# The last projection's last two tiles by three ranges of tokens, and a norm's squares added on VectorE

## The chip, the cores and the metric

The kernel runs on one core of a Trainium2 chip. The metric is the device time of one execution in microseconds, as the median of several runs. TensorE (PE in the profile) multiplies matrices, with a second row, PEld, for the loads of its stationary operand; VectorE is DVE, ScalarE is ACT, GpSimd is POOL, and SyncE (SP) issues most transfers. Each engine works through its own list of instructions in order; semaphores hold it where an operand is not there yet.

## The reference, cut to what matters

Two transformer blocks run one after the other on 512 tokens of 1024 channels. The change lies in the second block's feed-forward part:

```python
x = x + rms_norm(merged @ w_out[l], norm_mix_post[l])
h = rms_norm(x, norm_ffn_pre[l])                 # the squares of x are summed here
u = causal_dwconv(h @ w_up[l], conv_ffn_w[l])
a, g = jnp.split(u, 2, axis=-1)
f = (jax.nn.gelu(g, approximate=True) * a) @ w_down[l]     # 2816 -> 1024
x = x + rms_norm(f, norm_ffn_post[l])            # the last norm; x is the output
```

`rms_norm` divides each token by the root of the mean of its 1024 squares, so no element of a token can leave before all eight tiles of 128 channels of `f` are known for that token.

## The kernel before, in words

Activations lie transposed: a tile is 128 channels on the partitions by 512 tokens. A projection is cut into output tiles of 128 channels. Each tile sums over `nk` slices of 128 input channels in one PSUM bank; the down projection has `KF` = 22 slices. For accuracy every operand is split in a high and a low half (fp32r), and one slice is three matmuls (`mm3`, lines 163 to 165): high by high, low activation by high weight, high activation by low weight. The weights are the stationary operand (128x128), the activations `act` stream past in columns, one column for each token. Each matmul has its own weight load.

Weights come as pieces into `wraw`. `Stream.hi` lets ScalarE write the high half `whi` (line 201) and VectorE the low half `wlo` (line 209), up to two units ahead of TensorE (`AHEAD`); a unit is 8 or 6 slices of one tile. Nothing reorders this: the order in which the Python code is written is the order on each engine, and generators (`take`, `run`) interleave pieces of it.

The last projection is `ended_by_norm(p_down2, 1, ...)`. Tiles 0 to 6 are computed over all 512 tokens. After each, ScalarE copies the bank to `fo` with the norm's gain (`evac_f`, line 1543), and squares it (`square_o`, line 1473), and GpSimd adds the squares into `ssq` (line 1075). Tile 7 is done by halves of 256 tokens in one bank (`half`). Within the second half stand the sums over channels of the first half's squares (`col_sums`, line 382: matmuls against a column of ones, fp32, two passes each), the root (`rsqrt_col`, lines 319 to 329, VectorE with one square root on ScalarE), and its spread over the partitions (`bcast`, line 390, fp32, two passes for 128 tokens). Then `chain_f` multiplies `fo` by it (line 1550), adds the residual `x1` (line 1554), and sends the pieces out (lines 1556 and 1558). It gives one of the four pairs of tiles to GpSimd, and the second half's chain stands behind the first's. All that follows the last matmul of the second half is the end of the program.

The other place is `squares` (lines 1492 to 1499): between the second block's output projection and its up projection it squares the new `x1` on ScalarE (line 1497) and adds the squares of six tiles for each half of the tokens on GpSimd (line 1499). `start` (line 1503) puts the sums of these (`acc3`, `last3`) on TensorE in the midst of the up projection, and after nine more matmuls the spread root, which all the up projection's evacuations need.

Of the kernel before, what the change touches and what calls it, by code (L numbers as in the profile page):

```python
# [10 lines left out]
F32R = mybir.dt.float32r  # L11
AF = mybir.ActivationFunctionType
# [3 lines left out]
P = 128  # L16
T = 512
# [6 lines left out]
KF = FF // P  # L24
# [110 lines left out]
def program(ctx: ExitStack, tc: tile.TileContext, A, outT):  # L135
    nc = tc.nc
# [13 lines left out]
    def bank(name="bank", cols=T):  # L150
        return ps.tile([P, cols], F32, tag="b", name=name, padded_shape=[P, T])

    def slot(dt=F32, name="slot", cols=T):
        t = sl.tile([P, T], dt, tag="s", name=name)
        return t if cols == T else t[:, :cols]

    def pair(name, cols=T):
        return slot(F32R, name + "_hi", cols), slot(F32R, name + "_lo", cols)


    def mm3(out, lhs, rhs, start, stop, **kw):

        PE.matmul(out, lhs[0], rhs[0], start=start, stop=False, **kw)  # L163
        PE.matmul(out, lhs[0], rhs[1], start=False, stop=False, **kw)  # L164
        PE.matmul(out, lhs[1], rhs[0], start=False, stop=stop, **kw)  # L165
# [10 lines left out]
    class Stream:  # L176


        def __init__(self):
            self.pieces, self.units, self.raw, self.got, self.owed = [], [], [], [], []  # L180
            self.limit = 1 << 30
# [9 lines left out]
        def hi(self, u):  # L191

            while len(self.got) <= min(u, len(self.units) - 1):
                p, ks, cs = self.units[len(self.got)]
                self.load(p + 2)
                src = self.raw[p][:, ks, cs]
                nk, n = src.shape[1:]
                hi = whi_p.tile([P, 1024], F32R, tag="whi", name="whi")
                lo = wlo_p.tile([P, 1024], F32R, tag="wlo", name="wlo")
                h, l = (t[:, : nk * n].rearrange("p (k n) -> p k n", n=n) for t in (hi, lo))  # L200
                S.activation(h, src, AF.Copy)  # L201
                self.got.append((h, l))
                self.owed.append((l, src, h))
# [19 lines left out]
    class Proj:  # L223

        def __init__(self, w, c0, nk, ncol=256, wide=False):
            self.nk, self.at = nk, {}
            first = len(ws.pieces)
            segs = [(k0, min(8, nk - k0)) for k0 in range(0, nk, 8)]  # L230
            ws.pieces += [(w, k0, n, c0, ncol) for k0, n in segs]
            if wide:
                for u in range(0, nk, 4):
                    for k in range(4):
                        self.at[0, u + k] = (len(ws.units), k, 0)
                    ws.units.append((first, slice(u, u + 4), slice(0, ncol)))
                return
            per = 2 if nk <= 4 else 1
            for m in range(0, ncol // P, per):
                for s, (k0, n) in enumerate(segs):  # L240
                    for k in range(n):
                        for q in range(per):
                            self.at[m + q, k0 + k] = (len(ws.units), k, q * P)
                    ws.units.append((first + s, slice(0, n), slice(m * P, (m + per) * P)))
# [11 lines left out]
    def tiles(pj, ms, acts, evac):  # L256

        for m in ms:
            b = bank()
            yield from tile_gen(pj, m, acts, b)  # L260

            ws.hi(ws.early(pj.at[m, pj.nk - 1][0] + 1))
            evac(m, b)
            ws.lo()
            tick()

    def run(gen):
        for _ in gen:
            pass
# [104 lines left out]
    def sqrt_table():  # L374
        S.activation(warm, ones, AF.Sqrt)

    def col_sums(parts, blocks):

        b = bank("sums", cols=len(blocks))
        for i, blk in enumerate(blocks):  # L380
            for j, a in enumerate(parts):
                PE.matmul(b[:, i : i + 1], a[:, blk * P : (blk + 1) * P], ones,  # L382
                          start=(j == 0), stop=(j == len(parts) - 1))
        return b

    def bcast(col, n):

        b = bank("bc", cols=n * P)
        for i in range(n):
            PE.matmul(b[:, i * P : (i + 1) * P], col[:, i : i + 1].to_broadcast([P, P]), ident,  # L390
                      start=True, stop=True)
        return b
# [33 lines left out]
        ])  # L426
    p_out2 = [Proj(A["w_out_2"], 256 * i, 8) for i in range(4)]
    p_up2 = [[Proj(A["w_up_2"], c + 256 * j, 8) for c in (FF, 0)] for j in range(KF // 2)]
    p_down2 = [Proj(A["w_down_2"], 256 * i, KF) for i in range(4)]


    xs = []
# [10 lines left out]
    def pc(name, i, n=1):  # L443
        a = PCOL[name][0]
        return par[:, a + i : a + i + n]
# [613 lines left out]
    ws.limit = 1 << 30  # L1059


    def ended_by_norm(pjs, late, acts, evac, square, chain, follow=None, between=None, begun=(), after=None):


        nk = pjs[0].nk
        acc = slot(name="ssq")
        whole = 8 - late

        def early(m, b, i0):
            i = i0 + m  # L1070
            evac(i, b, slice(0, T))
            t = acc if i == 0 else slot(name="sq")
            square(i, t, b, slice(0, T))
            if i:
                G.tensor_add(acc, acc, t)

        for i, (g, b) in enumerate(begun):
            run(g)
            early(i, b, 0)
            tick()  # L1080
        for i in range(len(begun), whole):
            run(tiles(pjs[i // 2], (i % 2,), acts, lambda m, b: early(i % 2, b, i - i % 2)))
        if between:
            between()
        sqrt_table()
        ends = {i: (bank(), slot(name="sq")) for i in range(whole, 8)}

        def half(ts):
            for i in range(whole, 8):
                b, t = ends[i]  # L1090
                yield from tile_gen(pjs[i // 2], i % 2, acts, b, ts)
                evac(i, b, ts)
                square(i, t, b, ts)

        def sums(hf):
            return rsqrt_col(col_sums([acc] + [ends[i][1] for i in range(whole, 8)], (2 * hf, 2 * hf + 1)), 2)

        n = late * nk
        run(half(HALF[0]))
        g = half(HALF[1])  # L1100
        take(g, max(4, n // 4))
        r = sums(0)
        take(g, max(6, n // 4))
        bc = bcast(r, 2)
        ch = chain(0, HALF[0], bc)
        take(ch, CHN)
        run(g)
        run(ch)
        if follow is None:
            run(chain(1, HALF[1], bcast(sums(1), 2)))  # L1110
            return
        a, b = follow(HALF[0])
        run(a)
        r = sums(1)
        take(b, 4)
        ch = chain(1, HALF[1], bcast(r, 2))
        run(ch)
        if after:
            after(0)
        run(b)  # L1120
        a, b = follow(HALF[1])
        run(a)
        if after:
            after(1)

        ws.limit += 2
        ws.need(ws.limit - 2)
        run(b)
        ws.limit = 1 << 30
# [362 lines left out]
    def squares(hf):  # L1492
        ts = HALF[hf]
        for k in range(8):
            t = acc3 if k == 0 else last3 if k == 7 else slot(name="sq", cols=256)
            t = t[:, ts] if k in (0, 7) else t
            S.activation(t, x1[k][:, ts], AF.Square)
            if 0 < k < 7:
                G.tensor_add(acc3[:, ts], acc3[:, ts], t)  # L1499

    R3 = slot(name="R3")

# [30 lines left out]
    ffn_up(p_up2, (p_out2, 2, mg, evac_o, square_o, chain_o), h2, evac_g2, evac_a2, after=squares, start=start)  # L1533


    fo = {}

    def evac_f(i, b, ts):
        for hf in range(2):
            if ts.start <= HALF[hf].start < ts.stop:  # L1540
                if (i // 2, hf) not in fo:
                    fo[i // 2, hf] = slot(name="fo").rearrange("p (k n) -> p k n", k=2)
                S.activation(fo[i // 2, hf][:, i % 2, :], b[:, HALF[hf]], AF.Copy, scale=pc("norm_ffn_post_2", i))

    def chain_f(hf, ts, rb):
        rbs = slot(name="rbs", cols=256)
        out = outT.rearrange("(k p) n -> p k n", p=P)
        for j, e in ((0, V), (1, V), (3, G), (2, V)):
            f = fo[j, hf]
            e.tensor_mul(f, f, (rbs if j else rb).unsqueeze(1).to_broadcast([P, 2, 256]))  # L1550
            if j == 0:
                S.activation(rbs, rb, AF.Copy)
            for n in range(2):
                e.tensor_add(f[:, n, :], f[:, n, :], x1[2 * j + n][:, ts])
                if j == 2:
                    nc.sync.dma_start(out[:, 4 + n, ts], f[:, n, :])
            if j != 2:
                nc.sync.dma_start(out[:, 2 * j : 2 * j + 2, ts], f)
            yield j + 1

    ended_by_norm(p_down2, 1, act, evac_f, square_o, chain_f)


# [16 lines left out]
```

## Time and profile before

| | |
|---|---|
| median of 3 runs | 1421.41 us (1418.87 to 1423.46) |
| the profiled execution | 1421.66 us, its span 1419.9 us |
| TensorE busy | 1382.8 us, 97% of the span |
| VectorE, ScalarE, GpSimd busy | 55%, 39%, 16% |
| last matmul of the last projection starts | 1405.41 us |
| mean granted TensorE clock | 0.991 of 2.4 GHz |

Times in rows are microseconds from the start of the span. A matmul row's start is when it begins to stream, and the time between two starts is what a matmul costs in a full stream, since the end of one overlaps the next. In square brackets stands the idle time of the engine before the row, and who ended it.

### The profile page before, as it was taken

How to read it: one execution, taken by the hardware profiler on the slowest of the kernel's cores; microseconds unless marked ns; L12 is line 12 of the kernel's file. 1: busy time of each engine (PE TensorE's matmuls, PEld its weight loads, DVE VectorE, ACT ScalarE, POOL GpSimd, SP SyncE). 2: the span in 40 equal slices, each digit the busy share in tenths (PEclk: the TensorE clock that was granted, in tenths of full speed). 3: DMA queues.
4: the chain of work that ended last, by engine and by line, in shares of the span. 5: the costliest groups of instructions: out<-in, count | busy, mean ns of one | idle time of the engine just before them, and what ended most of it. 6: DMA issues, size and time to landing. Idle time of an engine off the chain costs nothing.

```text
span 1419.9 us, 18781 instructions
## 1 busy us (share of the span) xinstructions
PE 1382.8 (97%) x7546; PEld 1166.0 (82%) x7546; DVE 778.9 (55%) x1140; ACT 557.8 (39%) x892; POOL 221.1 (16%) x210
## 2 busy tenths in 40 slices
PE   6999999999999999999999999999999999999996
PEld 4767988899888888888988888888887888888886
DVE  4478777656444433443557874445257866663224
ACT  4433256535333333323345543223454534443321
POOL 0021324111110111112010212000261101110102
PEclk9999999999999999999999999999999999999998
DMA  9993252322322322232274123223311323222221
GB/s 364 342 338 107 78 148 58 121 89 89 119 89 89 119 88 83 82 104 90 59 201 112 60 68 111 89 89 111 98 60 60 119 90 114 94 82 82 93 71 60
DMA packets 141942, 160.42 MB, mean 113 GB/s; under 512 B 5664, under 2 KB 119584, under 8 KB 141856
## 3 DMA queue, kind: packets, MB, share of 16 engines
q1 hardware_dynamic: 140416, 156.91, 33.6%
q10 hardware_dynamic: 1440, 2.31, 0.5%
q8 instruction: 59, 0.97, 0.3%
q14 instruction: 27, 0.22, 0.0%
HBM read 147.67 MB, written 2.10 MB: 105 GB/s over the span
## 4 chain that ended last, share of the span: by engine, by line
PE 86%; DVE 7%; ACT 3%; issue 2%; DMA 1%; POOL 1%; SPq 0%; DVEq 0%; ACTq 0%; POOLq 0%
PE bank L164 24%; PE bank L163 24%; PE bank L165 24%; PE v L163 1%; PE v L165 1%; PE v L164 1%; PE sums L382 1%; PE first L163 1%; DVE wlo L209 1%; PE z L1362 1%; PE first L165 1%; PE first L164 1%; DVE e L887 1%; POOL acc L1499 1%; PE ada L472 1%
## 5 line engine op out<-in xcount | busy, mean ns | idle before, releaser
L209 DVE TENSOR_TENSOR wlo<-wraw,whi 128x1024 fp32r<-128x1024 f32 (+1 forms) x214 | 278.9, 1310 | 141.5 <-ACT whi L201 141.4
L164 PE MATMUL bank<-h_lo,whi 128*128 128x512 f32 (+1 forms) x816 | 306.3, 375 | 0.1
L163 PE MATMUL bank<-h_hi,whi 128*128 128x512 f32 (+1 forms) x816 | 305.7, 375 | 0.0
L165 PE MATMUL bank<-h_hi,wlo 128*128 128x512 f32 (+1 forms) x816 | 304.7, 373 | 0.8 <-DVE wlo L209 0.8
L201 ACT ACTIVATE whi<-wraw 128x1024 fp32r<-128x1024 f32 (+1 forms) x214 | 220.6, 1035 | 121.1 <-PE bank L164 107.0
L163 PEld LDWEIGHTS bank<-h_hi,whi 128*128 128x128 f32 x816 | 153.9, 189 | 30.4 <-PE adab L472 1.7
L165 PEld LDWEIGHTS bank<-h_hi,wlo 128*128 128x128 f32 x816 | 154.0, 189 | 28.6 <-DVE wlo L209 1.6
L164 PEld LDWEIGHTS bank<-h_lo,whi 128*128 128x128 f32 x816 | 153.9, 189 | 28.2 <-DVE h_lo L1490 0.3
L163 PE MATMUL bank<-act_hi,whi 128*128 128x512 f32 (+1 forms) x374 | 141.1, 377 | 0.8 <-ACT sq L1473 0.8
L164 PE MATMUL bank<-act_lo,whi 128*128 128x512 f32 (+1 forms) x374 | 140.8, 376 | 0.0
L165 PE MATMUL bank<-act_hi,wlo 128*128 128x512 f32 (+1 forms) x374 | 140.8, 376 | 0.0
L171 POOL TENSOR_TENSOR act_lo<-cv,act_hi 128x512 fp32r<-128x512 f32 x44 | 61.2, 1391 | 420.7 <-ACT act_hi L170 386.5
L163 PE MATMUL bank<-hb_hi,whi 128*128 128x512 f32 x288 | 115.8, 402 | 0.0
L165 PE MATMUL bank<-hb_hi,wlo 128*128 128x512 f32 x288 | 112.6, 391 | 0.0
L164 PE MATMUL bank<-hb_lo,whi 128*128 128x512 f32 x288 | 112.4, 390 | 0.0
L163 PEld LDWEIGHTS bank<-act_hi,whi 128*128 128x128 f32 x374 | 70.4, 188 | 14.0 <-ACT sq L1473 1.0
L165 PEld LDWEIGHTS bank<-act_hi,wlo 128*128 128x128 f32 x374 | 70.4, 188 | 13.0
L164 PEld LDWEIGHTS bank<-act_lo,whi 128*128 128x128 f32 x374 | 70.4, 188 | 12.7
L170 ACT ACTIVATE act_hi<-cv 128x512 fp32r<-128x512 f32 x44 | 27.8, 633 | 129.6 <-DVE cv L1204 73.0
L165 PEld LDWEIGHTS bank<-hb_hi,wlo 128*128 128x128 f32 x288 | 54.0, 188 | 11.5
L163 PEld LDWEIGHTS bank<-hb_hi,whi 128*128 128x128 f32 x288 | 54.2, 188 | 9.4
L164 PEld LDWEIGHTS bank<-hb_lo,whi 128*128 128x128 f32 x288 | 54.2, 188 | 9.0
(360 smaller groups left out, 2357.8 us busy)
## 6 DMA issues: line engine op xcount, KB each, us to landing
wraw<-in_w_in SPq DMA_DIRECT2D x23, 1024.0 KB, 5.4
wraw<-in_ffn_w_up SPq DMA_DIRECT2D x22, 1024.0 KB, 4.9
wraw<-in_w_up SPq DMA_DIRECT2D x22, 1024.0 KB, 4.9
ada<-in_ada_w SPq DMA_DIRECT2D x64, 256.0 KB, 5.5
ada<-in_ada_first SPq DMA_DIRECT2D x32, 256.0 KB, 5.8
wraw<-in_w_out SPq DMA_DIRECT2D x8, 1024.0 KB, 4.9
wraw<-in_ffn_w_down SPq DMA_DIRECT2D x8, 1024.0 KB, 4.8
wraw<-in_w_down SPq DMA_DIRECT2D x8, 1024.0 KB, 4.7
```

The costliest lines, as they stand in the source:

```text
L163: PE.matmul(out, lhs[0], rhs[0], start=start, stop=False, **kw)
L164: PE.matmul(out, lhs[0], rhs[1], start=False, stop=False, **kw)
L165: PE.matmul(out, lhs[1], rhs[0], start=False, stop=stop, **kw)
L170: S.activation(hi, src, AF.Copy)
L171: (eng or V).tensor_sub(lo, src, hi)
L201: S.activation(h, src, AF.Copy)
L209: V.tensor_sub(l, src, h)
L382: PE.matmul(b[:, i : i + 1], a[:, blk * P : (blk + 1) * P], ones, start=(j == 0), stop=(j == len(parts) - 1))
L472: PE.matmul(out[32 * g : 32 * g + 32, : rhs.shape[1]], sc[:, kk, :], rhs, start=start, stop=stop, tile_position=(0, 32 * g), skip_group_ch ...
L887: V.tensor_tensor_reduce(e, s, btile[(3 * (n // 4) + PAT[blk]) % 4], -1.0, 3e38, op0=ALU.add, op1=ALU.min, accum_out=nm)
L1362: PE.matmul(z, qs2[hp][a][j][:, b * P : (b + 1) * P], ks2[hp][j][:, :nk], start=a == 0, stop=a == 1)
L1499: G.tensor_add(acc3[:, ts], acc3[:, ts], t)
```

## The change

It makes three edits.

First, the last projection no longer uses `ended_by_norm`. Tiles 0 to 5 are computed over all tokens. Tiles 6 and 7 are computed together for tokens 0 to 255, then for 256 to 383, then for 384 to 511, each tile and range in a bank of its own (`part_gen`). The weights of tile 6 are split into units of four slices that go to slots of their own (`wk`) and stay until the third range; those of tile 7 stay in `whi` and `wlo`. The sums and the root of a range stand after 6 slices of the next range's tile 6, the spread root after 10 more.

Second, multiplying and adding at the end (`part_end`) is on VectorE alone, from PSUM, with no copy of the spread root; for the last range the residual is copied before into `xe`, so that one add covers four tiles. Output pieces are 2 tiles by 256 tokens, then 4 tiles by 128. Squaring comes before the copy in `part_gen`.

Third, the adds of `squares` go from GpSimd to VectorE.

```diff
-                p, ks, cs = self.units[len(self.got)]
+                p, ks, cs, *kept = self.units[len(self.got)]
...
+                if kept:
+                    hi, lo = pair("wk")
+                else:
...
+                    if m in kept:
+                        for u in range(0, n, 4):
+                            for k in range(u, min(u + 4, n)):
+                                self.at[m, k0 + k] = (len(ws.units), k - u, 0)
+                            ws.units.append((first + s, slice(u, min(u + 4, n)), slice(m * P, (m + 1) * P), slot))
+                        continue
...
-    p_down2 = [Proj(A["w_down_2"], 256 * i, KF) for i in range(4)]
+    p_down2 = [Proj(A["w_down_2"], 256 * i, KF, kept=(0,) if i == 3 else ()) for i in range(4)]
...
             if 0 < k < 7:
-                G.tensor_add(acc3[:, ts], acc3[:, ts], t)
+                V.tensor_add(acc3[:, ts], acc3[:, ts], t)
...
-    ended_by_norm(p_down2, 1, act, evac_f, square_o, chain_f)
+    PART = slice(0, 256), slice(256, 384), slice(384, 512)
+    BLOCKS = (0, 1), (2,), (3,)
...
+    for i in range(6):
+        run(tiles(p_down2[i // 2], (i % 2,), act, lambda m, b: evac_f(i, b)))
+    sqrt_table()
+    ends = {i: slot(name="sq") for i in (6, 7)}
+
+    def part_gen(s):
+        ts = PART[s]
+        for i in (6, 7):
+            b = bank("f", cols=ts.stop - ts.start)
+            for k in range(KF):
+                mm3(b, p_down2[3].part(i % 2, k), [a[:, ts] for a in act[k]], k == 0, k == KF - 1)
+                yield 3
+            S.activation(ends[i][:, ts], b, AF.Square)
+            S.activation(fo_of(s, i), b, AF.Copy, scale=pc("norm_ffn_post_2", i))
+
+    def part_root(s):
+        return rsqrt_col(col_sums((acc, ends[6], ends[7]), BLOCKS[s]), len(BLOCKS[s]))
+
+    def part_end(s, r):
+        ts = PART[s]
+        rb = bcast(r, len(BLOCKS[s]))
+        k0 = 0
+        for f in fo[s]:
+            n = f.shape[1]
+            V.tensor_mul(f, f, rb.unsqueeze(1).to_broadcast(list(f.shape)))
+            if s == 2:
+                V.tensor_add(f, f, xe[k0 // n])
+            else:
+                for k in range(n):
+                    V.tensor_add(f[:, k, :], f[:, k, :], x1[k0 + k][:, ts])
+            nc.sync.dma_start(out[:, k0 : k0 + n, ts], f)
+            k0 += n
+
+    run(part_gen(0))
...
+    for s in (1, 2):
+        g = part_gen(s)
+        take(g, 6)
+        r = part_root(s - 1)
+        take(g, 10)
+        part_end(s - 1, r)
+        run(g)
+    part_end(2, part_root(2))
```

On TensorE, before, around the sums of the first half, which stand in the second half of tile 7 (`bank` is the tile's PSUM bank, `ssq` the added squares of tiles 0 to 6, `sq` the last tile's):

```order
L164 MATMUL bank<-act_lo,whi 128x256
L165 MATMUL bank<-act_hi,wlo 128x256
L382 MATMUL sums<-ones,ssq 128x1
L382 MATMUL sums<-ones,sq 128x1
L382 MATMUL sums<-ones,ssq 128x1
L382 MATMUL sums<-ones,sq 128x1
L163 MATMUL bank<-act_hi,whi 128x256
```

And now, around the sums of the first range, in the second range of tile 6:

```order
L164 MATMUL f<-act_lo,wk_hi 128x128
L165 MATMUL f<-act_hi,wk_lo 128x128
L392 MATMUL sums<-ones,ssq 128x1
L392 MATMUL sums<-ones,sq 128x1 x2
L392 MATMUL sums<-ones,ssq 128x1
L392 MATMUL sums<-ones,sq 128x1 x2
L163 MATMUL f<-act_hi,wk_hi 128x128
```

The stream around the sums has matmuls of 128 columns where it had 256, and the sums are six matmuls where they were four. In all, tiles 6 and 7 had 66 matmuls of 512 columns and 132 of 256; they now have 132 of 256 and 264 of 128.

On VectorE, before, the end from the last root on (`bc` is the spread root in PSUM, `rbs` ScalarE's copy of it; one pair of tiles is on GpSimd's list):

```order
L329 SCALAR_TENSOR_TENSOR ro<-rt,rr 128x2
L1550 TENSOR_TENSOR fo<-fo,bc 128x512
L1554 TENSOR_TENSOR fo<-fo,x_0_3231 128x256
L1554 TENSOR_TENSOR fo<-fo,x_1_3233 128x256
L1550 TENSOR_TENSOR fo<-fo,rbs 128x512
L1554 TENSOR_TENSOR fo<-fo,x_2_3235 128x256
L1554 TENSOR_TENSOR fo<-fo,x_3_3237 128x256
L1550 TENSOR_TENSOR fo<-fo,rbs 128x512
L1554 TENSOR_TENSOR fo<-fo,x_4_3239 128x256
L1554 TENSOR_TENSOR fo<-fo,x_5_3241 128x256
```

And now:

```order
L339 SCALAR_TENSOR_TENSOR ro<-rt,rr 128x1
L1589 TENSOR_TENSOR fo<-fo,bc 128x512
L1591 TENSOR_TENSOR fo<-fo,xe 128x512
L1589 TENSOR_TENSOR fo<-fo,bc 128x512
L1591 TENSOR_TENSOR fo<-fo,xe 128x512
```

Nine instructions after the last root have become four, and GpSimd has none behind it.

## Rows read from the trace of the kernel before

**Rows 1.** The chain that ended last, by engine, from the page.
```profile
PE 86%; DVE 7%; ACT 3%; issue 2%; DMA 1%; POOL 1%; SPq 0%; DVEq 0%; ACTq 0%; POOLq 0%
```

**Rows 2.** Timeline at the norm's squares: start, duration, engine, line, operands [idle before].
```profile
1056.02 4.78 DVE L209 TENSOR_TENSOR wlo<-wraw,whi 128x1024 fp32r<-128x1024 f32 x3 [5.38 <-ACT whi L201]
...
1063.03 0.38 PE L382 MATMUL sums<-ones,acc 128*128 128x1 f32 x2 [2.15 <-POOL acc L1499]
...
1063.95 0.69 PE L163 MATMUL bank<-h_hi,whi 128*128 128x512 f32 x1
...
1067.42 0.41 PE L165 MATMUL bank<-h_hi,wlo 128*128 128x512 f32 x1
```

**Rows 3.** Timeline of TensorE in the last projection's tiles 6 and 7.
```profile
1372.33 0.39 PE L163 MATMUL bank<-act_hi,whi 128*128 128x512 f32 x1
...
1396.20 0.39 PE L163 MATMUL bank<-act_hi,whi 128*128 128x256 f32 x1 [0.84 <-ACT sq L1473]
...
1398.09 0.28 PE L382 MATMUL sums<-ones,ssq 128*128 128x1 f32 x2
...
1399.10 0.28 PE L164 MATMUL bank<-act_lo,whi 128*128 128x256 f32 x1
...
1401.13 0.60 PE L390 MATMUL bc<-ident,ro 128*128 128x128 f32 x4
...
1401.70 0.28 PE L164 MATMUL bank<-act_lo,whi 128*128 128x256 f32 x1
...
1405.41 0.28 PE L165 MATMUL bank<-act_hi,wlo 128*128 128x256 f32 x1
```

**Rows 4.** Timeline of TensorE: matmuls of 128 columns with 128x128 weights, second block's attention.
```profile
787.72 0.27 PE L1362 MATMUL z<-k_hi,q_hi 128*128 128x128 f32 x1
...
788.06 0.45 PE L163 MATMUL bank<-hb_hi,whi 128*128 128x512 f32 x1
```

**Rows 5.** Timeline of TensorE: one-column sums with 128x128 weights, pairs of passes.
```profile
684.53 0.36 PE L382 MATMUL sums<-ones,sq 128*128 128x1 f32 x2
...
687.65 0.36 PE L382 MATMUL sums<-ones,sq 128*128 128x1 f32 x2
```

**Rows 6.** Timeline of TensorE: nine matmuls of 128 columns with 128x64 weights.
```profile
841.54 0.22 PE L163 MATMUL o<-wt_hi,v_hi 128*64 128x128 f32 x1
...
842.08 0.44 PE L163 MATMUL bank<-hb_hi,whi 128*128 128x512 f32 x1
```

**Rows 7.** Timeline of ScalarE before tile 7's first half ends: the square root's table.
```profile
1388.83 1.28 ACT L375 ACT_TABLE_LOAD   x1
```

**Rows 8.** Timeline behind the last matmul.
```profile
1405.73 0.47 ACT L1543 ACTIVATE fo<-bank,par 128x256 f32<-128x256 f32 x1 [2.85 <-PE bank L165]
1406.10 0.38 ACT L1473 ACTIVATE sq<-bank 128x256 f32<-128x256 f32 x1
...
1408.01 0.15 DVE L319 TENSOR_SCALAR rv<-sums 128x2 f32<-128x2 f32 x1
...
1409.24 1.22 PE L390 MATMUL bc<-ident,ro 128*128 128x128 f32 x4 [1.88 <-DVE ro L329]
1410.50 0.69 DVE L1550 TENSOR_TENSOR fo<-fo,bc 128x512 f32<-128x512 f32 x1 [1.31 <-PE bc L390]
...
1411.90 1.75 DVE L1550 TENSOR_TENSOR fo<-fo,rbs 128x512 f32<-128x512 f32 x1
...
1416.01 0.76 DVE L1554 TENSOR_TENSOR fo<-fo,x 128x256 f32<-128x256 f32 x2
```

**Rows 9.** Output transfers of the last 30 us: size, median time to landing.
```profile
out_T<-fo SPq DMA_DIRECT2D x6, 256.0 KB, 2.3
out_T<-fo SPq DMA_DIRECT2D x4, 128.0 KB, 2.1
```

**Rows 10.** Stretches: length, busy time by engine, granted clock, DMA share, GB/s.
```profile
689.00:691.00 2.00, 2.00 (x11) 2.00 (x11) 1.44 (x8) 1.23 (x4) 0.00 (x0) 0.50 0.00 0
213.00:217.00 4.00, 3.49 (x40) 3.39 (x40) 3.15 (x11) 2.60 (x6) 1.74 (x3) 1.00 0.66 176
```

More of the change, by code (lines that the diff above doesn't have):

```diff
@@ L197, in hi @@
                 nk, n = src.shape[1:]
-                hi = whi_p.tile([P, 1024], F32R, tag="whi", name="whi")
-                lo = wlo_p.tile([P, 1024], F32R, tag="wlo", name="wlo")
+                if kept:
+                    hi, lo = pair("wk")
+                else:
+                    hi = whi_p.tile([P, 1024], F32R, tag="whi", name="whi")
+                    lo = wlo_p.tile([P, 1024], F32R, tag="wlo", name="wlo")
                 h, l = (t[:, : nk * n].rearrange("p (k n) -> p k n", n=n) for t in (hi, lo))
@@ L223, in program, with __init__ @@
     class Proj:
-        def __init__(self, w, c0, nk, ncol=256, wide=False):
+        def __init__(self, w, c0, nk, ncol=256, wide=False, kept=()):
             self.nk, self.at = nk, {}
@@ L1059, in program, with ended_by_norm @@
     ws.limit = 1 << 30
-    def ended_by_norm(pjs, late, acts, evac, square, chain, follow=None, between=None, begun=(), after=None):
+    def ended_by_norm(pjs, late, acts, evac, square, chain, follow, between=None, begun=(), after=None):
         nk = pjs[0].nk
@@ L1108, in ended_by_norm @@
         run(ch)
-        if follow is None:
-            run(chain(1, HALF[1], bcast(sums(1), 2)))
-            return
         a, b = follow(HALF[0])
@@ L1533, in program @@
     ffn_up(p_up2, (p_out2, 2, mg, evac_o, square_o, chain_o), h2, evac_g2, evac_a2, after=squares, start=start)
[L1536 to L1559, printed above, removed]
@@ L1561, in program, with fo_of @@
-    ended_by_norm(p_down2, 1, act, evac_f, square_o, chain_f)
+    PART = slice(0, 256), slice(256, 384), slice(384, 512)
+    BLOCKS = (0, 1), (2,), (3,)
+    out = outT.rearrange("(k p) n -> p k n", p=P)
+    acc = slot(name="ssq")
+    fo = []
+    for ts in PART:
+        n = ts.stop - ts.start
+        fo.append([slot(name="fo").rearrange("p (k n) -> p k n", n=n) for _ in range(8 * n // T)])
+    def fo_of(s, i):
+        per = fo[s][0].shape[1]
+        return fo[s][i // per][:, i % per, :]
@@ new lines, in evac_f @@
+    def evac_f(i, b):
+        for s, ts in enumerate(PART):
+            S.activation(fo_of(s, i), b[:, ts], AF.Copy, scale=pc("norm_ffn_post_2", i))
+        t = acc if i == 0 else slot(name="sq")
+        S.activation(t, b, AF.Square)
+        if i:
+            G.tensor_add(acc, acc, t)
+    for i in range(6):
[11 more added lines that the diff above has]
+            S.activation(fo_of(s, i), b, AF.Copy, scale=pc("norm_ffn_post_2", i))
@@ L1565 @@
+    run(part_gen(0))
+    xe = [slot(name="xe").rearrange("p (k n) -> p k n", n=P) for _ in range(2)]
+    for k in range(8):
+        S.activation(xe[k // 4][:, k % 4, :], x1[k][:, PART[2]], AF.Copy)
+    for s in (1, 2):
[6 more added lines that the diff above has]
+    part_end(2, part_root(2))
 def kernel(**inputs):
```

## The prediction

> **What bounds the kernel now.** The chain that ended last lies for 86% on TensorE [rows 1], so a change counts where it alters TensorE's stream or the tail behind the last matmul. I read three stretches of the timeline. At the norm's squares TensorE stands idle for 2.15 us until GpSimd has added them, and the eight matmuls behind it run from 1063.95 to 1067.42, 0.434 us each: the clock has fallen to its lower level [rows 2]. In the last projection tile 6 begins at 1372.33 and the last matmul starts at 1405.41, with one stall of 0.84 us, where tile 7's second half waits until ScalarE has read the bank [rows 3]. From 1405.41 to the span's end at 1419.9 are 14.5 us in which TensorE has only sums and the spread root, and VectorE most of the chain [rows 8].
>
> **The norm's squares.** Twelve adds leave GpSimd. On VectorE one costs about 0.38 us, half of the 0.76 us that two adds of 128x256 take [rows 8], so 4.6 us in all. VectorE is idle for 5.38 us there, since it waits for ScalarE's weight copies, which stand behind the squares on ScalarE [rows 2]; this idle time is the cover. If it did not reach, three weight splits of VectorE and then TensorE's next weights would be late. With the sums not waiting, 2.15 us go. Whether the clock stays up is not shown by before; the eight matmuls at the usual 0.227 us (66 of 512 columns from 1372.33 on, in 14.96 us) would be 1.65 us shorter. The idle time seems to be the cause, so I take both: -3.8 us, with -2.1 as the other end. The root that follows has nine matmuls to hide in, 2.0 us, and needs 1.23 us from the first step to the spread (1408.01 to 1409.24, [rows 8]), so nothing new waits there.
>
> **Three ranges: TensorE's stream.** This is the large term. Before, tiles 6 and 7 with sums, spread and stall take 1405.53 - 1372.33 = 33.2 us (one step of 0.12 us behind the last start). Now they are 132 matmuls of 256 columns and 264 of 128. For 256 columns the rows give 0.120 us (31 steps from 1401.70 to 1405.41, [rows 3]): 15.8 us. For 128 columns halving would be the naive price, but the trace shows two things against it. Three matmuls of 128 columns with full 128x128 weights took 0.34 us, 0.113 each [rows 4]. And a pass of one single column with such weights costs as much: 14 pairs of passes from 684.53 to 687.65 are 0.1114 us a pass [rows 5]. So below some 250 columns it is the load of the weights, one for each matmul, that sets the pace. I take 0.112 us: 264 x 0.112 = 29.6 us, with ends at 0.111 (one column) and 0.120 (256 columns), 29.3 and 31.7 us. Only where the weights are half as wide do 128 columns run faster: nine of them in 0.54 us, 0.060 each [rows 6]; the change's weights are full.
>
> The Trainium skill, page "TensorE: Matmul & The Clock Gate", section "Back-to-back issue gap", states for a stream of load and matmul pairs about 81 ns at 128 columns. The rows of this kernel with full weights do not agree (0.113 us); by that figure the 264 would take 21.4 us and the sum below would come out 8.2 us lower, at 1419.2.
>
> Sums and spread stand inside the stream. Eight passes of sums cost 1399.10 - 1398.09 less one step, 0.89 us, and four passes of the spread 0.45 us [rows 3]. Now there are 12 and 6 passes of sums and 4 and 2 of the spread: 1.33 + 0.67 + 0.45 + 0.23 = 2.7 us. The sums wait for a square that was given 6 slices earlier, 2.0 us; the spread comes 10 slices, 3.4 us, after its root was begun and needs 1.23: no wait. Banks of their own remove the 0.84 us, which is in the 33.2. Together 15.8 + 29.6 + 2.7 = 48.1 us, or +14.9.
>
> One thing can be late: the square root's table, 1.28 us on ScalarE [rows 7], now stands ahead of the fourth to sixth weight unit of tile 6, after tile 5's evacuation. TensorE has twelve slices, 4.3 us, until it needs the fourth. That is about what evacuation, table, copy and VectorE's half take; I put 0.2 us, with ends 0 and 1.3. What VectorE does for the first range (four multiplies of 0.69 and eight adds of 0.38, 5.8 us) lies beside 28 slices of TensorE, 9.4 us, and for the second range it is less, so VectorE is free when the last root comes. SP has nothing but output pieces left in its queue, and GpSimd only five adds, long done.
>
> **The tail.** Now: 0.32 us from the last start to ScalarE [rows 3, 8]; a square of 128 columns, 0.29 (0.38 for 256, taken between 0.20 and 0.38), where before the copy came first; 0.43 for the last pair of sums to VectorE's first step; 1.23 to the spread; for two passes instead of four 0.7 (1.26 for four at the lower clock, so 0.4 to 1.26); two multiplies and two adds, 2 x (0.69 + 0.76) = 2.9. Before, it was three pairs, one multiply of which took 1.75 us while GpSimd was on its own pair [rows 8]. From VectorE's end (1416.77) to the span's end were 3.13 us; the last piece is now 256 KB instead of 128, 0.2 us more by the time to landing [rows 9], at most 0.9: 3.3. Sum 9.2 instead of 14.5, so -5.3 us (ends -4.1 and -5.7).
>
> **Sum.** -3.8 + 14.9 + 0.2 - 5.3 = +6.0 us. The profiled execution took 1421.66 us, 1.76 more than its span and 0.25 above the median; on the median of 1421.41 it gives 1427.4. With all ends at their best +5.1 (1426.5), with all at their worst +12.1 (1433.5).
>
> **Rivals.** (1) The weights of the next matmul load behind the one that runs, and 128 columns cost the 0.060 us of half-wide weights [rows 6]: 264 x 0.052 = 13.7 us less, 1413.7, faster. It needs full weights to load in half the time of rows 4 and 5; those rows speak against it. It decides from 0.081 us on: there the sum is 1419.2, no longer slower, the value of the page named above. Chance 0.04 for 1413.7 and 0.04 for about 1419.
> (2) The clock falls and stays. After the one-column sums of 684 to 688 it stood at 0.50, eleven matmuls in 2 us [rows 10]: weight loads alone did not hold it. The change puts 12 such passes between matmuls that stream for about half of their step (0.060 of 0.112). In favour of the clock speaks the stretch from 213 to 217 us, forty mostly 128-column matmuls with idle time among them, at 1.00 [rows 10]. A short fall, as before, would cost 1 to 2 us, which I count to the forecast. If the thin stream cannot lift it again, some 250 matmuls cost twice 0.112: +27 us, 1454. Chance 0.08.
> (3) The twelve adds do not fit into VectorE's idle time, the weight splits come late, and the norm's 3.8 us are given back: 1431.2. Against it speak the 5.38 us. Chance 0.07.
>
> **How the numbers follow.** The forecast has 0.77, its time 1427.4 us. The difference that a measurement of this kernel can tell from none is 0.3%, 4.3 us: slower means over 1425.7, faster under 1417.1. Of the forecast's 0.77 I give 0.10 to times below 1425.7 (terms at their best and a spread of runs of 2 us). Slower: 0.67 + 0.08 + 0.07 = 0.82, lowered to 0.80 for what I have not seen; the same 0.15; faster 0.05. The range from 1419 to 1434 holds the forecast with a short fall of the clock, rival 3 and the upper half of rival 1; it leaves out 1413.7 and 1454.
>
> **What would show it.** In the changed kernel's timeline 128-column matmuls of `f` at steps of 0.11 us, tile 6's start to the last start about 48 us apart; at steps of 0.06 to 0.08 rival 1 holds. The granted clock at 0.5 through ranges two and three is rival 2. Behind the up projection's sums no idle time ended by GpSimd, and the matmuls there at 0.23 us. The tail from the last start about 9 us. I would be wrong if TensorE did not load weights for each matmul, or if a wait for `wk` appeared in the first range.

## The result, and the profile after

The changed kernel takes 1452.93 us (median of 4 runs, 1451.19 to 1456.91) beside 1420.14 of the kernel before (4 runs): a ratio of 1.0229, interval 1.0208 to 1.0251. The forecast was 1427.4 with a range of 1419 to 1434. So the direction came out as forecast, the size did not: the profiled execution (1454.58 us, span 1452.7) lies 27 us above the sum. Rival 2 of the prediction, priced at 1454 us, had got a chance of 0.08.

The stretches of the changed kernel around its last projection show where the 27 us are. Columns: stretch, its length, busy time and number of instructions of PE, PEld, DVE, ACT and POOL, then the granted clock, the DMA share and GB/s.

```profile
1385.00:1387.00 2.00, 2.00 (x21) 2.00 (x19) 0.00 (x0) 1.74 (x8) 0.00 (x0) 1.00 0.00 0
...
1388.00:1389.00 1.00, 1.00 (x10) 1.00 (x10) 0.28 (x2) 0.20 (x1) 0.00 (x0) 0.92 0.00 0
1389.00:1391.00 2.00, 2.00 (x11) 2.00 (x11) 0.53 (x4) 0.00 (x0) 0.00 (x0) 0.50 0.00 0
...
1431.00:1441.00 10.00, 10.00 (x49) 10.00 (x48) 0.00 (x0) 0.00 (x0) 0.00 (x0) 0.50 0.01 2
```

TensorE's busy share is 100% in every row. What changes is the clock, from 1.00 to 0.50 (2.4 to 1.2 GHz), and with it the count: 21 instructions in 2 us before 1387, 11 in 2 us behind 1389, and 49 in 10 us still forty to fifty microseconds later. A busy share alone hides this loss; the count of instructions and the clock column show it.

TensorE's timeline of the changed kernel at the place of the fall (start, duration, engine, line, operands, size of the weights, columns, count):

```profile
1385.00 0.22 PE L163 MATMUL f<-act_hi,wk_hi 128*128 128x128 f32 x1
...
1385.18 0.27 PE L165 MATMUL f<-act_hi,wk_lo 128*128 128x128 f32 x1
...
1386.85 0.27 PE L165 MATMUL f<-act_hi,wk_lo 128*128 128x128 f32 x1
1386.96 0.33 PE L392 MATMUL sums<-ones,ssq 128*128 128x1 f32 x2
1387.15 0.59 PE L392 MATMUL sums<-ones,sq 128*128 128x1 f32 x4
1387.60 0.36 PE L392 MATMUL sums<-ones,ssq 128*128 128x1 f32 x2
1387.82 0.59 PE L392 MATMUL sums<-ones,sq 128*128 128x1 f32 x4
1388.27 0.30 PE L163 MATMUL f<-act_hi,wk_hi 128*128 128x128 f32 x1
...
1389.08 0.42 PE L163 MATMUL f<-act_hi,wk_hi 128*128 128x128 f32 x1
...
1393.99 0.41 PE L165 MATMUL f<-act_hi,wk_lo 128*128 128x128 f32 x1
...
1442.63 0.41 PE L165 MATMUL f<-act_hi,wlo 128*128 128x128 f32 x1
```

From 1385.18 to 1386.85 there are 15 steps in 1.67 us, 0.111 us for a matmul of 128 columns. Twelve one-column passes follow. From 1389.08 to 1393.99 there are 23 steps in 4.91 us, 0.2135 us each, and that pace stays to the last start at 1442.63.

### The profile page after: what moved, and what is told of

It reads as the page before. It is cut to its first block, busy times and chain, and to the rows that moved or that the text cites. A ratio compares the mean times of both kernels' runs of the same rounds, so it can differ in the third digit from the quotient of the medians.

```text
span 1452.7 us, 19206 instructions
## 1 busy us (share of the span) xinstructions
PE 1423.6 (98%) x7752; PEld 1211.2 (83%) x7752; DVE 781.7 (54%) x1168; ACT 560.4 (39%) x913; POOL 201.4 (14%) x191
## 4 chain that ended last, share of the span: by engine, by line
PE 87%; DVE 6%; ACT 3%; DMA 2%; issue 2%; POOL 1%; SPq 0%; DVEq 0%; ACTq 0%; POOLq 0%
PE bank L164 22%; PE bank L163 22%; PE bank L165 22%; PE f L165 2%; PE f L164 2%; PE f L163 2%; PE sums L392 1%; PE v L163 1%; PE v L165 1%; PE v L164 1%; DVE wlo L212 1%; PE first L163 1%; PE z L1369 1%; PE first L165 1%; PE first L164 1%
## 5 line engine op out<-in xcount | busy, mean ns | idle before, releaser
L212 DVE TENSOR_TENSOR wlo<-wraw,whi 128x1024 fp32r<-128x1024 f32 (+1 forms) x211 | 272.9, 1301 | 116.3 <-ACT whi L204 116.1
L204 ACT ACTIVATE whi<-wraw 128x1024 fp32r<-128x1024 f32 (+1 forms) x211 | 217.5, 1036 | 105.9 <-PE bank L164 91.8
L165 PEld LDWEIGHTS bank<-h_hi,wlo 128*128 128x128 f32 x816 | 153.7, 188 | 29.3 <-DVE wlo L212 2.3
L163 PE MATMUL bank<-act_hi,whi 128*128 128x512 f32 x308 | 120.0, 389 | 0.0
L164 PE MATMUL bank<-act_lo,whi 128*128 128x512 f32 x308 | 120.0, 389 | 0.0
L165 PE MATMUL bank<-act_hi,wlo 128*128 128x512 f32 x308 | 119.9, 389 | 0.0
L164 PEld LDWEIGHTS bank<-act_lo,whi 128*128 128x128 f32 x308 | 57.9, 188 | 12.1
L165 PEld LDWEIGHTS bank<-act_hi,wlo 128*128 128x128 f32 x308 | 57.8, 188 | 12.0
L163 PEld LDWEIGHTS bank<-act_hi,whi 128*128 128x128 f32 x308 | 57.9, 188 | 11.9
```

The source lines that it names most:

```text
L212: V.tensor_sub(l, src, h)
```

## The experiments

Theory A: two things together cost the time. Twelve one-column passes in one piece, between matmuls of 128 columns, bring the clock down, and a stream of 128-column matmuls that would have held the clock does not bring it back. Rival B: the 128-column stream falls by itself, without the passes. Rival C: once down, the clock stays down whatever streams.

**No passes in the stream.** All sums, spreads and outputs stand behind the last matmul.

```diff
     for s in (1, 2):
-        g = part_gen(s)
-        take(g, 6)
-        r = part_root(s - 1)
-        take(g, 10)
-        part_end(s - 1, r)
-        run(g)
-    part_end(2, part_root(2))
+        run(part_gen(s))
+    for s in range(3):
+        part_end(s, part_root(s))
```

> The changed kernel with all three ranges' sums, roots, broadcasts and outputs behind the last matmul, so that the 264 matmuls of 128 columns run with nothing between them. Theory A (the cluster of 12 one-column passes takes the clock down, and the 128-column stream, which holds it, cannot bring it back) expects a granted clock of 1.00 to the last matmul: 1369.1 + 15.9 + 264 x 0.111 (29.3) = 1414.3 for the last start; then the sums of three ranges, about 24 passes (2.7 us), the chain to the first broadcast, VectorE's outputs (5.5 + 2.8 + 2.8) and the last transfer, some 18 us in all: about 1434 us. Rival B (a stream of 128-column matmuls is too thin by itself, without the passes) expects the clock to fall to 0.50 a few us into it: up to 264 x 0.2135 = 56.4 in place of 29.3, about 1460 us.

Measured: 1438.81 us in one run. Stretches of this kernel, columns as above:

```profile
1391.00:1401.00 10.00, 10.00 (x92) 10.00 (x91) 0.00 (x0) 1.07 (x4) 0.00 (x0) 1.00 0.01 2
1401.00:1411.00 10.00, 10.00 (x92) 10.00 (x91) 0.00 (x0) 0.54 (x2) 0.00 (x0) 1.00 0.00 0
```

The first and the last thin matmul, from the same kernel's timeline of TensorE:

```profile
1384.50 0.22 PE L163 MATMUL f<-act_hi,wk_hi 128*128 128x128 f32 x1
...
1413.82 0.28 PE L165 MATMUL f<-act_hi,wlo 128*128 128x128 f32 x1
```

The clock is 1.00 through all 264 thin matmuls: from 1384.50 to the last start at 1413.82 are 29.3 us, 0.111 each, as expected. Rival B has fallen. The time is 5 us over the expected 1434, because the three outputs in a row behind the last matmul came to 23 us, not 18.

**The passes spread.** One sums matmul (two passes) after every nine matmuls of the next range.

```diff
-        r = part_root(s - 1)
+        blks = BLOCKS[s - 1]
+        sb = bank("sums", cols=len(blks))
+        for i, blk in enumerate(blks):
+            for j, a in enumerate((acc, ends[6], ends[7])):
+                PE.matmul(sb[:, i : i + 1], a[:, blk * P : (blk + 1) * P], ones, start=(j == 0), stop=(j == 2))
+                take(g, 3)
+        r = rsqrt_col(sb, len(blks))
```

> The changed kernel with the sums of ranges 0 and 1 not in a cluster but one matmul (two one-column passes) after every nine matmuls of the next range. Theory A (the cluster): the clock holds at 1.00, and the time is the one forecast for the whole change, about 1427 us. Rival B (the 128-column stream alone falls): clock 0.50 for nearly the whole of the 128-column part, as in the changed kernel, about 1453 us.

> The changed kernel with the sums' passes spread over the stream, now timed. One look gave 1424.4 beside 1423.3 of before, where the forecast for the whole change at full clock was 1427.4 beside 1421.4. By the forecast's sum: a ratio of 1.0042. By the one look: 1.0008.

Measured: 1424.36 us in a first single run; timed, 1428.70 us (4 runs, 1428.37 to 1430.39) beside 1422.13 of before (29 runs), a ratio of 1.0051, interval 1.0034 to 1.0069. Two stretches of the timed kernel, columns as above:

```profile
1391.00:1401.00 10.00, 10.00 (x91) 10.00 (x91) 3.37 (x11) 0.63 (x3) 0.00 (x0) 1.00 0.02 8
1401.00:1411.00 10.00, 10.00 (x92) 10.00 (x91) 3.77 (x13) 1.28 (x5) 0.00 (x0) 1.00 0.28 99
```

The first matmul of tile 6 and the last one of the stream, from the same kernel's timeline of TensorE:

```profile
1369.11 0.28 PE L163 MATMUL f<-act_hi,wk_hi 128*128 128x256 f32 x1
...
1416.99 0.28 PE L165 MATMUL f<-act_hi,wlo 128*128 128x128 f32 x1
```

The same matmuls and the same eighteen passes, only spread, and the clock stays at 1.00 to the last start: 24 us less than the changed kernel. The cluster is the cause of the fall.

**The stream widened.** The cluster of passes is as in the changed kernel; every matmul of ranges 1 and 2 runs over 256 columns, and the half that is not needed is not used.

```diff
-            b = bank("f", cols=ts.stop - ts.start)
+            b = bank("f", cols=256)
+            w = HALF[min(s, 1)]
...
-                mm3(b, p_down2[3].part(i % 2, k), [a[:, ts] for a in act[k]], k == 0, k == KF - 1)
+                mm3(b, p_down2[3].part(i % 2, k), [a[:, w] for a in act[k]], k == 0, k == KF - 1)
...
+            b = b[:, ts.start - w.start : ts.stop - w.start]
```

> The changed kernel, same ranges, same cluster of passes, same evacuations, but every matmul of the two 128-token ranges streams 256 columns (both ranges' tokens; the half that isn't needed is computed and not used). Theory A: with 256 columns to a matmul the clock stays at 1.00 or comes back within some 4 us of the passes, so that twice the columns take less time than half of them: 264 x 0.120 = 31.7 in place of the 55 us measured for the 128-column part, tail as in the changed kernel: 1369.1 + 15.9 + 31.7 + about 3.5 for the sums and broadcasts + 10.1 + 1.9 = 1432 us, 1434 with a dip. Rival C (the passes put the clock down for good): 264 matmuls of 256 columns at half clock, at least 0.22 each, 58 us: about 1458 us or more.

Measured: 1431.05 us in one run. TensorE's timeline at the cluster, the first pass and the first matmul behind the last:

```profile
1387.72 0.28 PE L392 MATMUL sums<-ones,ssq 128*128 128x1 f32 x2
...
1388.98 0.36 PE L163 MATMUL f<-act_hi,wk_hi 128*128 128x256 f32 x1
```

The stretches around it, columns as above:

```profile
1388.00:1389.00 1.00, 1.00 (x11) 1.00 (x11) 0.00 (x0) 0.15 (x1) 0.00 (x0) 1.00 0.00 0
1389.00:1391.00 2.00, 2.00 (x19) 2.00 (x19) 0.81 (x5) 0.20 (x1) 0.00 (x0) 1.00 0.00 0
1391.00:1401.00 10.00, 10.00 (x86) 10.00 (x85) 5.53 (x12) 0.54 (x2) 0.00 (x0) 1.00 0.31 106
```

The same twelve passes in 1.26 us, and the clock does not fall at all. TensorE streams twice the columns in these two ranges, and its last matmul starts 23 us earlier (at 1419.76 in place of 1442.63).

**Only the last range widened.** This asks what brings the clock back.

```diff
-            b = bank("f", cols=ts.stop - ts.start)
+            w = HALF[1] if s == 2 else ts
+            b = bank("f", cols=w.stop - w.start)
...
-                mm3(b, p_down2[3].part(i % 2, k), [a[:, ts] for a in act[k]], k == 0, k == KF - 1)
+                mm3(b, p_down2[3].part(i % 2, k), [a[:, w] for a in act[k]], k == 0, k == KF - 1)
...
+            b = b[:, ts.start - w.start : ts.stop - w.start]
```

> The changed kernel with its cluster of 12 passes in the 128-column stream as it is, and only the last range's 132 matmuls widened to 256 columns (the half that isn't needed is computed and not used). Theory A, its second half (at the low clock a 128-column stream cannot lift the clock, a 256-column one can): clock 0.50 from the cluster through the second range, as in the changed kernel, and back at 1.00 within some 4 us of the last range's start; the last range then 132 x 0.120 = 15.9 us and about 1.5 for the low start in place of 132 x 0.2135 = 28.2: 1453 - 11 = 1442 us. Rival (once down, the clock comes back only after TensorE has rested, whatever streams): 132 x 0.24 or so, 1455 us or more, 0.50 to the end.

Measured: 1441.35 us in one run. Stretches of this kernel; its last range begins at 1412.62:

```profile
1386.00:1387.00 1.00, 1.00 (x11) 1.00 (x10) 0.00 (x0) 0.80 (x5) 0.00 (x0) 1.00 0.00 0
1389.00:1411.00 22.00, 22.00 (x105) 22.00 (x104) 5.52 (x12) 0.54 (x2) 0.00 (x0) 0.50 0.14 49
1411.00:1414.00 3.00, 3.00 (x15) 3.00 (x15) 0.00 (x0) 0.54 (x2) 0.00 (x0) 0.50 0.00 0
1414.00:1415.00 1.00, 1.00 (x7) 1.00 (x7) 0.00 (x0) 0.00 (x0) 0.00 (x0) 0.57 0.00 0
1415.00:1417.00 2.00, 2.00 (x20) 2.00 (x19) 0.16 (x1) 0.20 (x1) 0.00 (x0) 1.00 0.00 0
```

TensorE's timeline of this kernel behind 1412.62, still at the low clock:

```profile
1412.94 0.41 PE L164 MATMUL f<-act_lo,wk_hi 128*128 128x256 f32 x1
...
1414.44 0.41 PE L165 MATMUL f<-act_hi,wk_lo 128*128 128x256 f32 x1
```

The clock falls behind the cluster as in the changed kernel, stays at 0.50 through 22 us of 128-column matmuls without a gap, and is back at 1.00 some 2 us after the 256-column matmuls begin. Rival C has fallen, and the second half of A stands, by this one run. TensorE was fully busy on both sides of 1412.62; only the columns of a matmul changed, while the changed kernel, with 128 columns from there on, stayed at 0.50 to its last matmul.

**Six passes in one piece.** The spread kernel with range 1's three sums matmuls together again.

```diff
+        if s == 2:
+            r = part_root(1)
+            take(g, 10)
+            part_end(1, r)
+            run(g)
+            break
```

> The spread kernel, but the last cluster back in one piece: range 0's six sums matmuls spread as before, range 1's three (six one-column passes) together, three slices of them earlier than in the changed kernel's place. Theory A (it is how many passes stand together in a thin stream that counts): if half the changed kernel's first cluster is still enough, the clock falls about 1 us behind it and stays at 0.50: some 114 matmuls at 0.2135 in place of 0.111, +11.7 us and 1 for the second broadcast, about 1441 us. If six passes are too few, 1428 us and a clock of 1.00 to the last matmul. I expect the second with 0.6.

Measured: 1428.36 us in one run. The stretches with the six passes, which begin at 1403.33, and behind them:

```profile
1403.00:1405.00 2.00, 2.00 (x20) 2.00 (x20) 1.36 (x7) 0.20 (x1) 0.00 (x0) 1.00 0.48 166
1405.00:1407.00 2.00, 2.00 (x20) 2.00 (x20) 0.28 (x2) 0.00 (x0) 0.00 (x0) 1.00 0.29 100
```

The clock is 1.00 to the last matmul of the stream. (The six passes stand where the changed kernel has them; the expectation's "three slices earlier" was a slip.) In this run six passes were harmless; nothing between six and twelve was tried.

**The parts that were meant to gain.** Three kernels: the norm's edit alone on the kernel before; that plus outputs on VectorE alone in the old two halves; and the changed kernel with two ranges of 256 tokens.

```diff
-                G.tensor_add(acc3[:, ts], acc3[:, ts], t)
+                V.tensor_add(acc3[:, ts], acc3[:, ts], t)
```
```diff
-        for j, e in ((0, V), (1, V), (3, G), (2, V)):
+        for j, e in ((0, V), (1, V), (3, V), (2, V)):
```
```diff
-    PART = slice(0, 256), slice(256, 384), slice(384, 512)
-    BLOCKS = (0, 1), (2,), (3,)
+    PART = slice(0, 256), slice(256, 512)
+    BLOCKS = (0, 1), (2, 3)
...
```

> The kernel before with only the norm's edit: its six additions of squares on VectorE in place of GpSimd. Theory A (the norm's edit is worth what the trace of after shows, 3.85 us from the sums to the broadcast, and nothing of it is given back): 3.8 us less than before, a ratio of 0.9973. Rival (the gain is given back where VectorE or the weight split is late next, the prediction's rival 3): a ratio of 1.000.

> The kernel before with the norm's edit and, in its own two halves, the one output pair that GpSimd multiplied and added now on VectorE; tiles, banks and order as before. Theory (two engines on the outputs at once slow each other: a 512-element product took VectorE 1.75 us beside GpSimd's and 0.69 alone, so VectorE alone loses nothing): tail from the broadcast on 4 x (0.69 + 0.76) = 5.8 us in place of 6.3, and -3.8 of the norm: -4.3 us, a ratio of 0.9970. If GpSimd's share was a help, VectorE's two more instructions to a half cost 1.45 us in the tail: -2.4, a ratio of 0.9983.

> The changed kernel with two ranges of 256 tokens in place of 256, 128 and 128: the last projection's stream is 264 matmuls of 256 columns, with the same 12 one-column passes in it. Theory A (the 128-column stream is what the clock does not come back from) expects a granted clock of 1.00 over the stream but for a few us behind the passes: stream 264 x 0.120 = 31.7 us, sums and wait 1.3, broadcast about 1; tail longer than the changed kernel's 10.1 us by eight VectorE instructions of 512 elements (8 x 0.69 = 5.5 in place of 2.8) and six more passes, about 13.8. From tile 6's start at 1369.1: 1369.1 + 34 + 13.8 + 1.9 = 1418 us, 1421 with a dip of the clock. Rival C (the 12 passes, or what the kernel did before them, put the clock down for good, whatever streams behind): half of the stream at half the clock, 132 x about 0.22 = 29 in place of 15.9: 1431 to 1433 us.

> The two-range kernel again, now timed: the norm's edit, two ranges of 256 tokens, outputs on VectorE alone. By the one look (1416.8 us beside 1423.3 of before) a ratio of 0.9954. By rows: norm -3.8; the stream 264 x 0.120 as it was; the tail 13.2 us behind the last matmul's start in place of 14.5: -1.3. Sum -5.1, a ratio of 0.9964. If the first look was a matter of the chip's day and the norm is all there is: 0.9973.

Measured, 12 runs each beside 1422.13 us of before (29 runs): the norm alone 1418.50, a ratio of 0.9980 (0.9967 to 0.9992); with the outputs on VectorE 1419.06, 0.9977 (0.9964 to 0.9990); two ranges 1417.87, 0.9968 (0.9955 to 0.9981), after 1416.78 in a first single run. All three beat the kernel before by 0.2 to 0.3%. The intervals overlap, so their order stays open.

The traces say a little more than the times. The multiply that took 1.75 us beside GpSimd [rows 8] is there again in VectorE's timeline of the kernel with the norm's edit alone:

```profile
1403.60 0.69 DVE L1550 TENSOR_TENSOR fo<-fo,bc 128x512 f32<-128x512 f32 x1 [1.31 <-PE bc L390]
...
1405.00 1.75 DVE L1550 TENSOR_TENSOR fo<-fo,rbs 128x512 f32<-128x512 f32 x1
...
1409.11 0.76 DVE L1554 TENSOR_TENSOR fo<-fo,x 128x256 f32<-128x256 f32 x2
```

The same rows of the kernel with the outputs on VectorE alone:

```profile
1403.81 0.69 DVE L1550 TENSOR_TENSOR fo<-fo,bc 128x512 f32<-128x512 f32 x1 [1.16 <-PE bc L390]
...
1405.21 0.68 DVE L1550 TENSOR_TENSOR fo<-fo,rbs 128x512 f32<-128x512 f32 x1
...
1408.72 0.76 DVE L1554 TENSOR_TENSOR fo<-fo,x 128x256 f32<-128x256 f32 x2
```

From the first multiply to the last add it is 6.27 us with GpSimd's help and 5.67 without: that engine's quarter of the work was paid for by VectorE's slower instructions beside it. The times of the two kernels do not show this 0.6 us. In the two-range kernel the clock is 1.00 through the stream with its twelve passes, as it was in the widened one.

## Why the prediction was wrong in its size

*The norm, -3.8 us: right in its gain, but the cover fell short.* The place of [rows 2] in the changed kernel, on VectorE:

```profile
1050.94 6.05 DVE L1506 TENSOR_TENSOR acc<-acc,sq 128x256 f32<-128x256 f32 x12
1056.90 3.49 DVE L212 TENSOR_TENSOR wlo<-wraw,whi 128x1024 fp32r<-128x1024 f32 x3
```

On TensorE there:

```profile
1058.18 0.50 PE L165 MATMUL bank<-h_hi,wlo 128*128 128x512 f32 x1 [0.23 <-DVE wlo L212]
...
1060.60 0.28 PE L392 MATMUL sums<-ones,acc 128*128 128x1 f32 x2
...
1064.48 1.05 PE L400 MATMUL bc<-ident,ro 128*128 128x128 f32 x8
```

The sums and the spread before:

```profile
1059.94 0.28 PE L382 MATMUL sums<-ones,acc 128*128 128x1 f32 x2
...
1067.67 1.05 PE L390 MATMUL bc<-ident,ro 128*128 128x128 f32 x8
```

From the sums' start to the spread's are 3.88 us in the changed kernel, where before they were 7.73, so -3.85. The clock stays at 1.00 there, which the prediction had taken and not shown. But the twelve adds took 6.05 us and not 4.6, more than the 5.38 us of idle time that were to cover them. So VectorE has no idle time left ahead of the weight splits, these begin later (1056.90 against 1056.02), and one matmul of TensorE waits for them. The step ahead of it takes 0.63 us and the one behind it 0.34, where the others there take 0.23: about 0.5 us are given back, which is rival 3 in small, and -3.3 remain. The run with the edit alone has the same wait. Its measured gain is 2.8 us (0.2% of 1422, with 1.1 to 4.7 by the interval), which holds the forecast and excludes rival 3's nothing.

*Range 0, 132 x 0.120: right.* Tile 6 starts at 1369.13 and the first thin matmul at 1385.00, 15.87 us against 15.8 + 0.2; no table stall appeared.

*128 columns at 0.112 us: right at full clock*, 0.111 measured. So rival 1 did not happen, and the 0.081 us that the Trainium skill gives for 128 columns ("TensorE: Matmul & The Clock Gate", "Back-to-back issue gap") is not what this stream of full-width weights does, in any of the runs here.

*Sums between the ranges: right.* 1386.96 to 1388.27 for the first twelve passes, 1.31 against 1.33.

*The clock: wrong, and this is the step that failed.* The prediction named the mechanism and its price (+27) in rival 2, and then gave it 0.08 for the stretch from 213 to 217 us [rows 10], where 128-column matmuls ran at 1.00. That row does not bear on the question. Of its forty matmuls 24 have weights of 128x64, as these:

```profile
214.07 0.22 PE L164 MATMUL o<-pt_lo,v_hi 128*64 128x128 f32 x1
...
214.66 0.22 PE L165 MATMUL o<-pt_hi,vc_lo 128*64 128x128 f32 x1
```

Ten steps in 0.59 us are 0.059 each, the half-wide price of [rows 6] that the prediction itself had kept apart from the change's. Eight of the others have 256 columns, so only eight are of the change's size. That a thin stream with weights of 128x128 can keep a clock that is up was shown only by the kernels made afterwards, the one without passes over 29 us. That it survives twelve passes, or recovers from them, no row of before showed. Nor did the prediction look at what had ended the fall in the other row, at 689 us [rows 10]: it took "a short fall, as before" as the ordinary case. TensorE's timeline of before shows what ended it:

```profile
689.38 0.41 PE L163 MATMUL v<-whi,hb_hi 128*128 128x256 f32 x1
...
692.09 0.27 PE L164 MATMUL v<-wlo,hb_hi 128*128 128x256 f32 x1
```

The clock of the kernel before came back under matmuls of 256 columns, the very ones that the change takes away at its own place. One fall of before does have 128-column matmuls behind it, at 225 us, and its clock was back by 228. They have half-wide weights again, and four matmuls of 256 columns follow them. First two of these matmuls, then two stretches, columns as above:

```profile
225.79 0.31 PE L164 MATMUL o<-pt_lo,v_hi 128*64 128x128 f32 x1
...
226.86 0.31 PE L165 MATMUL o<-pt_hi,vc_lo 128*64 128x128 f32 x1
```
```profile
226.00:227.00 1.00, 1.00 (x12) 1.00 (x11) 0.72 (x3) 0.80 (x3) 0.27 (x1) 0.50 0.00 0
228.00:229.00 1.00, 1.00 (x17) 1.00 (x16) 0.93 (x3) 0.14 (x1) 0.94 (x1) 1.00 0.00 0
```

Ten steps in 1.07 us, 0.107 each, at a granted clock of 0.50: half of the 0.2135 that 128 columns took with full weights at this clock. So what is shown here of the thin stream is shown for weights of 128x128 alone, with one load for each matmul. With a row that spoke for the fall and none that spoke against it, 0.08 was far too little, and a range that ended at 1434 left the case out.

*The accounts.* From tile 6's start to the last start it is 73.5 us in place of 48.0, +25.5. About 241 matmuls ran behind the fall, at 0.2135 - 0.111 more each: 24.7; the second sums and both spreads at the low clock make up the rest. Tile 6 begins 0.6 later than the sum had it: 0.5 are TensorE's wait at the norm's weight splits, and before that wait this execution was 0.15 behind. The tail of the changed kernel, from the timeline:

```profile
1443.08 0.28 ACT L1577 ACTIVATE sq<-f 128x128 f32<-128x128 f32 x1 [13.55 <-PE f L165]
...
1445.54 0.80 PE L400 MATMUL bc<-ident,ro 128*128 128x128 f32 x2 [1.32 <-DVE ro L339]
```

From the last start (1442.63) to the span's end (1452.7) it took 10.1 us against 9.2 forecast and 14.5 before; sums at the low clock are part of the rest. 25.5 + 0.6 + 0.9 is 27.0; less the 0.2 for the table stall that did not appear it is the 26.8 us between the span forecast (1419.9 + 6.0) and the span measured.

*With the clock up, the sum holds.* The spread kernel is the changed kernel without the fall: 47.9 us from tile 6's start to the last start (1369.11 to 1416.99) against 48.0, a tail of 9.5 against 9.2, and 1428.7 us against 1427.4. So even then the change would have lost 0.5%. At full clock, two ranges of 128 columns cost 264 x 0.111 = 29.3 us for what one range of 256 does in 15.8, 13.5 more; the two-range kernel's tail is 13.1 (from the last start at 1402.48 to 1415.6) against 9.5, so the third range buys 3.6 us of tail with them.

*What stays open.* How many passes in one piece a 128-column stream bears between six and twelve, and whether their place in it matters. Why columns and weight loads move the clock as they do; no run looks behind that, and the widened streams and the six passes were run once each. The order of the three kernels that beat the one before.

## What to carry to other kernels

Before a matmul is cut along its columns, price it by a row of the same weights: below 256 columns the price hardly fell here (0.111 us at 128, 0.120 at 256). Where a stream is thin, spread small matmuls over it rather than set them in one piece, and look behind every place where the clock falls for what brings it back: here 24 us hung on where eighteen passes stood. The size of the weights belongs to such a row as much as its columns do. Read the clock and the number of instructions beside the busy share, since a TensorE at half speed shows as 100% busy.

## What was not expected of the hardware

A TensorE without any gap stayed at a granted clock of 0.50 for 53 us, from 1389 to the last start. In the run with the last range widened it came back within some 2 us once its matmuls had 256 columns in place of 128. At the low clock both widths took the same time, 0.2135 us for 128 columns and 0.214 for 256 (seven steps from 1412.94 to 1414.44), so with weights of 128x128 the thin matmul had no advantage at all there. And work that is thrown away paid: with 128 needless columns in each of 264 matmuls the kernel took 1431.05 us (one run) in place of 1452.93.
